# Chunked attention of one layer: both heads of a pair group by group, one split and one store for both

## Chip, cores and metric

The kernel runs on one core of a Trainium2 chip. The metric is the time of one launch on the device, in microseconds, as the median of several runs; the profile is that of one execution.

## The reference

One encoder layer on 1024 tokens of width 1024, in float32: a SwiGLU feed-forward block, then two attention mixers side by side, then a second feed-forward block. The change touches mixer A: attention with 8 heads of 64 columns, in chunks of 64 tokens; a token sees its own chunk and the 8 before it, with a bias for each distance.

```python
def _mixer_a(q, k, v, rel_bias):            # 8 heads of 64
    ...
    s = jnp.einsum('bnqhd,bnkhd->bnhqk', qc, kb) * (Dh ** -0.5)
    ...
    s = jnp.where(valid, s + bias[None, None], -jnp.inf)
    p = jax.nn.softmax(s, axis=-1)
    o = jnp.einsum('bnhqk,bnkhd->bnqhd', p, vb)
    return o.reshape(B, S, H * Dh)
```

After it, o_A is multiplied by a weight, gated, and added to what mixer B gives. Mixer B takes for each token the 256 best keys of an indexer (top-k).

## The kernel before, in words

All engines are programmed as tiles with dependencies; a planner puts the instructions of each engine in an order, by priority and by its own model of time. A tile with a tag has a fixed number of buffers (`bufs`); a new tile of the tag waits until an old one is free. Values are carried as two parts, high and low, so that products come out nearly exact: `split` (line 81) makes both, a ScalarE cast for the high part (line 82) and a VectorE subtraction for the low one (line 83). All DMAs are issued by SyncE (`dma`, line 79), in order.

Mixer A (`mixer_a`, line 698) works on four pairs of heads. For each pair, `load` (line 713) projects queries and keys with 128 columns each, and moves them into the tiles of each head: `qt0`, `qt1` (queries, high and low part stacked), `kk0`, `kk1` (keys, high part twice), `kl0`, `kl1` (low part twice), and `v0`, `v1` (values). Each of these tiles has one buffer. Each head has a bias tile `rb` (line 748), loaded by a DMA, with two small GpSimd memsets (lines 750 and 751); the tag has two buffers.

The loop then goes over the two heads (j), and in a head over four groups (g) of two blocks of 128 tokens (b). For a block, `score_chunks` (line 470, products at 480 and 481) writes the scores into a PSUM bank S (three of them), in one or two chunks; `softmax` (line 632) adds the bias and takes the maximum (VectorE, 639), then the exponential (ScalarE, 641), the reciprocal of its sum (VectorE, 642) and the scaling of the probabilities (GpSimd, 643). A block sees 1, 2, 3, 4, 5, 5, 5, 5 key tiles, so that the four groups have 3, 7, 10 and 10. The probability tile `p` has six buffers, so three groups of a head are on their way at most. `weighted` (line 646) turns the probabilities round on TensorE (665), splits them (tiles `pth`, `ptl`), and multiplies by the values into the bank pv (673). `halves` (line 677) adds the upper and the lower 64 partitions of pv: a ScalarE copy to the tile `half` (683) and a VectorE add to `ot` (684). `split` then makes the tile `os`, and a DMA stores it into `oa_d`. For head 0 this is on partitions 0 to 63, for head 1 on 64 to 127.

Two kinds of other work are woven in. `step` (in `filler`, line 990) is called after each block with its number of key tiles: it pays 0.34 filler steps for each (`pump`, line 134: six products of a projection, the next pair's `load` first, then tiles of the gates), and 0.2 steps of the top-k search. Both are planned at lower priority: the filler 250 instructions later, the search 5000 later. At the end of a pair the kernel pumps until the next pair's `load` is complete. When the stage is over, its pool is closed and the projections of mixer B (`proj_b`, line 788) begin in the same space.

Of the kernel before, what the change touches and what calls it, by code (L numbers as in the profile page):

```python
# [9 lines left out]
F32 = mybir.dt.float32  # L10
F32R = mybir.dt.float32r
# [8 lines left out]
P = 128  # L20
SEQ = 1024
D = 1024
NT = SEQ // P
# [3 lines left out]
HD = 64  # L27
# [10 lines left out]
SPAN_A = 640  # L38
# [5 lines left out]
class Layer:  # L44
# [653 lines left out]
    def mixer_a(self, hh, hl, w_in, va_d, oa_d, step):  # L698
        nc = self.nc
        pool, es = self.open("mxa", bufs=1)  # L700
# [39 lines left out]
        for pr in range(4):  # L740
            qt, kk, kl, vs = nxt
            nxt = []
            if pr < 3:
                self.finish()
                self.fill.appendleft(load(pr + 1, nxt))
            for j in range(2):
                r = j * HD
                bt = pool.tile([P, SPAN_A], F32, tag="rb", name=self.uid("rb"), bufs=2)
                self.dma(bt, self.io["rel"][2 * pr + j])
                nc.gpsimd.memset(bt[0:HD, SPAN_A - HD:SPAN_A], NEG)  # L750
                nc.gpsimd.memset(bt[HD:P, 0:HD], NEG)
                for g in range(NT // 2):
                    sides = []
                    for b in (2 * g, 2 * g + 1):
                        k0 = max(0, b - 4)
                        w = (b + 1 - k0) * P
                        tok = slice(b * P, (b + 1) * P)
                        span = slice(k0 * P, (b + 1) * P)
                        s = self.score_chunks(w, qt[j][:, tok], kk[j][:, span], kl[j][:, span])
                        p = pool.tile([P, SPAN_A], F32, tag="p", name=self.uid("p"), bufs=6)[:, :w]  # L760
                        sides.append((self.softmax(s, bt[:, SPAN_A - w:], p), k0, b + 1))
                        step(b + 1 - k0)
                    pv = self.bank("pv")
                    self.weighted(pv, sides, lambda k: vs[j][:, k, :], pool, 4)
                    ot = pool.tile([P, 256], F32, tag="ot", name=self.uid("ot"))[r:r + HD]
                    os_ = pool.tile([P, 2, 256], F32R, tag="os", name=self.uid("os"), bufs=1)[r:r + HD]
                    self.halves(ot, pv[:, :256], r, pool)
                    self.split(os_[:, 0, :], os_[:, 1, :], ot)
                    self.dma(oa_d[r:r + HD, pr, :, g * 256:(g + 1) * 256], os_)
            while pr < 3 and not nxt:  # L770
                self.pump(1)
        es.close()
# [352 lines left out]
```

## Time and profile before

| | us |
|---|---|
| median of 3 runs | 2391.39 (2390.85 to 2392.74) |
| profiled execution, device time | 2389.99 |
| its span, first to last instruction | 2388.2 |
| TensorE busy in the span | 2265.6 (95%) |
| VectorE busy | 1517.9 (64%) |
| ScalarE busy | 1010.3 (42%) |
| GpSimd busy | 589.8 (25%) |

The engines of a row are PE (TensorE; PEld is its weight load), DVE (VectorE), ACT (ScalarE), POOL (GpSimd) and SP (SyncE, which issues the DMAs). Starts are microseconds from the start of the span. "L82" is line 82 of the kernel. Mixer A's attention lies between about 984 and 1265 us.

### The profile page before, as it was taken

To read this page: it belongs to the slowest core of one execution; us is meant where nothing else is said; L and a number is where in the kernel's file an instruction comes from. 1 tells how busy PE (TensorE), PEld (TensorE's weight loads), DVE (VectorE), ACT (ScalarE), POOL (GpSimd) and SP (SyncE) were. 2 spreads that over 40 slices of the span, in tenths; PEclk is the share of its full clock that TensorE was granted. 3 is DMA by queue.
4 is the path that set the end of the run, shared out by engine and by line. 5 is a ranking of instruction groups with operands and counts; after the bars stand their busy time and mean duration, and the time that the engine had idled before them with its cause. 6 is when DMAs were issued, how large, how long until landed. Compare 5 with 4: busy or idle time off the path is not lost. (4 is left out here: it accounts for less than half of the span.)

```text
span 2388.2 us, 30574 instructions
## 1 busy us (share of the span) xinstructions
PE 2265.6 (95%) x10928; PEld 1893.1 (79%) x10928; DVE 1517.9 (64%) x2917; ACT 1010.3 (42%) x1971; POOL 589.8 (25%) x492
## 2 busy tenths in 40 slices
PE   4999999999998999899998999999799999999998
PEld 3877777778887988687778888878688888878886
DVE  7555555456657459798895378677655555546565
ACT  5444444410104454667743377633444444431012
POOL 6433333100005000223220043221733343300000
PEclk7999999999999999899999999999799999999999
DMA  4233333354414023455523241373233333354331
GB/s 134 89 106 106 106 106 106 106 203 159 159 71 146 1 80 98 131 127 136 126 71 103 87 159 49 112 250 110 89 106 115 106 106 106 106 218 169 132 142 71
DMA packets 204217, 280.82 MB, mean 118 GB/s; under 512 B 12064, under 2 KB 150304, under 8 KB 203552
## 3 DMA queue, kind: packets, MB, share of 16 engines
q1 hardware_dynamic: 204064, 278.86, 35.9%
q8 instruction: 86, 1.41, 0.3%
q14 instruction: 67, 0.55, 0.1%
HBM read 186.55 MB, written 79.69 MB: 111 GB/s over the span
## 5 line engine op out<-in xcount | busy, mean ns | idle before, releaser
L226 DVE SCALAR_TENSOR_TENSOR x<-S,x 128x512 f32<-128x512 f32 x400 | 270.6, 689 | 201.6 <-PE S L118 200.8
L83 DVE TENSOR_TENSOR wop<-raw,wop 128x512 fp32r<-128x512 f32 x210 | 150.3, 723 | 204.5 <-ACT wop L82 203.9
L82 ACT CAST whi<-raw 128x1024 fp32r<-128x1024 f32 (+1 forms) x90 | 85.6, 974 | 413.9 <-PE S L118 335.8
L335 PE MATMUL mm<-bigA,wop 128*128 128x512 f32 (+1 forms) x736 | 236.4, 384 | 10.6 <-ACT e L357 10.6
L335 PE MATMUL S<-bigA,wop 128*128 128x512 f32 (+1 forms) x736 | 235.1, 382 | 5.3 <-POOL wop L83 4.1
L118 PE MATMUL S<-wlo,goh 128*128 128x512 f32 x608 | 236.8, 389 | 0.0
L118 PE MATMUL S<-whi,gol 128*128 128x512 f32 x608 | 236.7, 389 | 0.0
L118 PE MATMUL S<-whi,goh 128*128 128x512 f32 x608 | 232.9, 393 | 1.9 <-DVE bigB L83 1.5
L82 ACT CAST wop<-raw 128x512 fp32r<-128x512 f32 x224 | 137.4, 625 | 103.7 <-PE mm L335 44.9
L335 PEld LDWEIGHTS mm<-bigA,wop 128*128 128x128 f32 x736 | 136.6, 188 | 46.0 <-ACT e L357 19.8
L118 PE MATMUL mm<-bigA,whi 128*128 128x512 f32 x384 | 156.0, 406 | 16.0 <-ACT whi L82 10.0
L83 DVE TENSOR_TENSOR wop<-s,wop 128x512 fp32r<-128x512 f32 x84 | 91.5, 1090 | 115.7 <-ACT wop L82 115.4
L335 PEld LDWEIGHTS S<-bigA,wop 128*128 128x128 f32 x736 | 137.6, 190 | 32.7 <-POOL wop L83 4.5
L118 PE MATMUL mm<-bigA,wlo 128*128 128x512 f32 x384 | 155.2, 405 | 2.1 <-POOL wlo L83 2.1
L118 PE MATMUL mm<-bigB,whi 128*128 128x512 f32 x384 | 154.9, 403 | 0.2 <-DVE bigB L83 0.2
L643 POOL TENSOR_SCALAR p<-p,z 128x640 f32<-128x640 f32 (+7 forms) x128 | 92.5, 726 | 211.8 <-DVE z L642 143.9
L83 POOL TENSOR_TENSOR wlo<-raw,whi 128x1024 fp32r<-128x1024 f32 (+1 forms) x32 | 67.7, 2114 | 301.1 <-ACT whi L82 292.3
L335 PE MATMUL S<-bigB,wop 128*128 128x512 f32 (+1 forms) x368 | 140.4, 382 | 0.1
L335 PE MATMUL mm<-bigB,wop 128*128 128x512 f32 (+1 forms) x368 | 139.8, 380 | 0.0
L118 PEld LDWEIGHTS S<-whi,goh 128*128 128x128 f32 x608 | 114.1, 188 | 31.5 <-DVE x L226 6.3
L309 POOL TENSOR_TENSOR raw<-raw,s 128x512 f32<-128x512 f32 x42 | 54.6, 1300 | 332.4 <-DVE wop L83 332.4
L335 PE MATMUL mm<-b,wop 128*128 128x512 f32 (+1 forms) x552 | 134.5, 381 | 0.0
(257 smaller groups left out, 5375.4 us busy)
## 6 DMA issues: line engine op xcount, KB each, us to landing
raw<-in_ffn_w_in_dram SPq DMA_DIRECT2D x88, 512.0 KB, 4.1
g_d<-g SPq DMA_DIRECT2D x80, 512.0 KB, 5.0
raw<-in_ffn_w_out_dram SPq DMA_DIRECT2D x44, 512.0 KB, 6.9
goh<-g_d SPq DMA_DIRECT2D x38, 512.0 KB, 5.2
gol<-g_d SPq DMA_DIRECT2D x38, 512.0 KB, 6.1
raw<-in_w_in_dram SPq DMA_DIRECT2D x28, 512.0 KB, 5.4
x<-in_x_dram SPq DMA_DIRECT2D x16, 512.0 KB, 7.5
x_d<-x SPq DMA_DIRECT2D x16, 512.0 KB, 2.6
```

The costliest lines, as they stand in the source:

```text
L82: self.nc.scalar.copy(hi, src)
L83: (eng or self.nc.vector).tensor_tensor(lo, src, hi.bitcast(F32), ALU.subtract)
L118: nc.tensor.matmul(out, lhsT=a, rhs=b, start=(i == 0), stop=(i == len(steps) - 1))
L226: nc.vector.scalar_tensor_tensor(xs, po, scale, xs, ALU.mult, ALU.add)
L309: nc.gpsimd.tensor_tensor(out, x, y, op)
L335: nc.tensor.matmul(out, lhsT=l, rhs=r, start=start and j == 0, stop=j == len(steps) - 1, skip_group_check=True)
L643: nc.gpsimd.tensor_scalar(p, p, z, 1.0, ALU.mult, ALU.mult)
```

## The change

The loop over the groups is now the outer one and the loop over the two heads the inner one. Both bias tiles of a pair are made ahead of the groups. The tiles `ot` and `os` belong to the group and not to the head: each head's `halves` writes its 64 partitions of `ot`, and after the second head one `split` on 128 partitions and one store follow. What is computed is the same, and so are the numbers of scores, softmaxes, products and filler steps.

```diff
@@ mixer_a
+            bts = []
             for j in range(2):
-                r = j * HD
                 bt = pool.tile([P, SPAN_A], F32, tag="rb", name=self.uid("rb"), bufs=2)
                 self.dma(bt, self.io["rel"][2 * pr + j])
                 nc.gpsimd.memset(bt[0:HD, SPAN_A - HD:SPAN_A], NEG)
                 nc.gpsimd.memset(bt[HD:P, 0:HD], NEG)
-                for g in range(NT // 2):
+                bts.append(bt)
+            for g in range(NT // 2):
+                ot = pool.tile([P, 256], F32, tag="ot", name=self.uid("ot"))
+                os_ = pool.tile([P, 2, 256], F32R, tag="os", name=self.uid("os"), bufs=1)
+                for j in range(2):
+                    r = j * HD
                     sides = []
                     for b in (2 * g, 2 * g + 1):
...
-                        sides.append((self.softmax(s, bt[:, SPAN_A - w:], p), k0, b + 1))
+                        sides.append((self.softmax(s, bts[j][:, SPAN_A - w:], p), k0, b + 1))
                         step(b + 1 - k0)
                     pv = self.bank("pv")
                     self.weighted(pv, sides, lambda k: vs[j][:, k, :], pool, 4)
-                    ot = pool.tile([P, 256], F32, tag="ot", name=self.uid("ot"))[r:r + HD]
-                    os_ = pool.tile([P, 2, 256], F32R, tag="os", name=self.uid("os"), bufs=1)[r:r + HD]
-                    self.halves(ot, pv[:, :256], r, pool)
-                    self.split(os_[:, 0, :], os_[:, 1, :], ot)
-                    self.dma(oa_d[r:r + HD, pr, :, g * 256:(g + 1) * 256], os_)
+                    self.halves(ot[r:r + HD], pv[:, :256], r, pool)
+                self.split(os_[:, 0, :], os_[:, 1, :], ot)
+                self.dma(oa_d[:, pr, :, g * 256:(g + 1) * 256], os_)
             while pr < 3 and not nxt:
                 self.pump(1)
```

## Rows read from the trace of the kernel before

**Rows 1.** The page, busy time, share of the span and instructions of each engine.

```profile
PE 2265.6 (95%) x10928; PEld 1893.1 (79%) x10928; DVE 1517.9 (64%) x2917; ACT 1010.3 (42%) x1971; POOL 589.8 (25%) x492
```

**Rows 2.** Busy time by stretch: start:end, length, engines (x instructions), clock, DMA share, GB/s.

```profile
984.00:1270.00 286.00, 261.45 (x1406) 219.60 (x1404) 255.41 (x728) 176.03 (x383) 79.86 (x90) 0.97 0.43 113
...
1180.00:1270.00 90.00, 82.29 (x418) 67.37 (x417) 87.65 (x189) 40.83 (x87) 20.96 (x18) 0.96 0.27 81
```

**Rows 3.** Timeline: start, duration, instruction, count, [idle before <-releaser]; end of the stage.

```profile
1268.84 0.69 DVE L629 TENSOR_SCALAR sc<-tkk 128x1024 f32<-128x1024 f16 x1
...
1272.99 1.74 PE L118 MATMUL S<-wb,bigA 128*128 128x384 f32 x4 [4.08 <-ACT wb L82]
```

**Rows 4.** Instructions of the tile os (ns min/median/max); idle ahead of them (us, times).

```profile
L82 ACT CAST os<-ot x32: 397/403/410, 1012.0 to 1262.6; 64x256 fp32r<-64x256 f32 x32
L83 DVE TENSOR_TENSOR os<-ot,os x32: 403/421/2272, 1014.5 to 1264.0; 64x256 fp32r<-64x256 f32 x32
L79 SPq DMA_DIRECT2D oa_d<-os x32: 574/599/2115, 1014.9 to 1264.5; - x32
...
  DVE ot L684: 21.1, 13
  DMA oa_d<-os: 3.1, 3
```

**Rows 5.** Busy time of the tile os alone in one stretch: VectorE, then ScalarE.

```profile
1180.00:1270.00 90.00, 8.30 (x11) 4.04 (x10) 0.96 0.27 81
```

**Rows 6.** Timeline of ScalarE: four of its 32 copies of half.

```profile
1009.97 0.37 ACT L683 COPY half<-pv 64x256 f32<-64x256 f32 x1 [0.22 <-PE pv L673]
...
1127.55 0.36 ACT L683 COPY half<-pv 64x256 f32<-64x256 f32 x1
...
1136.08 0.37 ACT L683 COPY half<-pv 64x256 f32<-64x256 f32 x1
...
1255.71 0.36 ACT L683 COPY half<-pv 64x256 f32<-64x256 f32 x1
```

**Rows 7.** Timeline of TensorE, two stalls; and ten microseconds by stretch around the second.

```profile
994.25 0.79 PE L118 MATMUL mm<-bigA,whi 128*128 128x512 f32 x1 [4.63 <-ACT whi L82]
...
1092.48 0.58 PE L673 MATMUL pv<-pth,v 128*128 128x256 f32 x1 [3.51 <-ACT pth L82]
...
1090.00:1100.00 10.00, 7.38 (x36) 6.54 (x36) 7.81 (x27) 7.19 (x16) 3.18 (x2) 0.83 0.46 98
```

**Rows 8.** Timeline of SyncE's DMA issues between the second and the third pair.

```profile
1094.76 1.20 SPq L79 DMA_DIRECT2D kk<-pwhi  x2
...
1102.03 0.46 SPq L79 DMA_DIRECT2D kk<-pwhi  x1
...
1107.68 1.33 SPq L79 DMA_DIRECT2D kl<-pwlo  x1
...
1125.61 0.34 SPq L79 DMA_DIRECT2D v<-va_d  x1
```

**Rows 9.** Timeline of TensorE there: last score, next scores, last product of the values.

```profile
1101.84 0.28 PE L481 MATMUL S<-kl,qt 128*128 128x256 f32 x1
...
1106.87 0.28 PE L481 MATMUL S<-kl,qt 128*128 128x256 f32 x1
...
1125.31 0.27 PE L673 MATMUL pv<-ptl,v 128*128 128x128 f32 x1
```

**Rows 10.** DMA issues from 984 to 1270: count, KB each, median us to landing.

```profile
kl<-pwlo SPq DMA_DIRECT2D x14, 256.0 KB, 4.8
...
v<-va_d SPq DMA_DIRECT2D x6, 512.0 KB, 3.6
rb<-in_rel_dram SPq DMA_DIRECT2D x6, 320.0 KB, 4.6
```

**Rows 11.** Timeline of GpSimd there: scaling of the second and the third block.

```profile
1112.04 0.48 POOL L643 TENSOR_SCALAR p<-p,z 128x256 f32<-128x256 f32 x1 [3.94 <-PE S L480]
...
1117.63 1.25 POOL L643 TENSOR_SCALAR p<-p,z 128x384 f32<-128x384 f32 x2
```

## Prediction

> **What bounds the kernel now.** I read the engine totals first [rows 1]: TensorE is busy 2265.6 of 2388.2 us, VectorE 1517.9, ScalarE 1010.3. TensorE is the bound over the whole run, and the change takes nothing from TensorE. So the change can only pay by shortening stretches in which TensorE stands idle, and only in the stage it touches. I then read the busy time of that stage [rows 2]. Mixer A runs from the first score at 984 us to the last store at about 1264.5 us; from 984 to 1270 TensorE is busy 261.45 of 286 us, so 24.5 us are idle, and that is the ceiling of any gain. VectorE is busy 255.41 of the same 286. Its last 90 us are different from the rest: from 1180 to 1270 VectorE is busy 87.65 of 90 while TensorE is busy 82.29. There VectorE is the bound, because the last steps of the top-k search have piled up in front of the attention's own subtractions; the last top-k instruction starts at 1268.84 [rows 3]. After that the next projection starts with TensorE idle for 4.08 us [rows 3]. A shorter VectorE queue in these 90 us moves that start, and everything behind it; TensorE's idle there, 90 - 82.29 = 7.7 us, is the most it can give.
>
> Next, the instructions that the change removes, by their tile [rows 4]. There are 32 ScalarE casts (median 403 ns), 32 VectorE subtractions (median 421 ns, but up to 2272 ns) and 32 stores, each on 64 partitions. ScalarE waited 21.1 us for VectorE ahead of 13 of the casts and 3.1 us for an earlier store ahead of 3. Of VectorE's 32 subtractions, 11 lie between 1180 and 1270, and they took 8.30 us in sum [rows 5].
>
> Last, the rhythm of the stage, from ScalarE's copies of the output half [rows 6], one per head and group, 32 in all. The first stands at 1009.97 and the last at 1255.71: 245.74 / 31 = 7.93 us for one group of one head, and groups with 3 key tiles take hardly less than groups with 10.
>
> **The change part by part.**
>
> *Split and store once per group.* Half of the casts, subtractions and stores go: 16 of each. An instruction on 128 partitions and the same 256 columns replaces two on 64. How long it takes is not shown for this tile; I take the same 0.40 and 0.42 us, since the columns are the same (bound: double, which would remove the gain of this part entirely). ScalarE is then freed of 16 x 0.403 = 6.4 us and VectorE of 16 x 0.421 = 6.7 us. Where this lands matters. Of the 11 subtractions in the VectorE-bound stretch about 5.5 go: 5.5 x 0.421 = 2.3 us by the median, 8.30 / 2 = 4.15 us by what they took there. The long ones are single instructions caught behind something else, which will then catch another instruction, so I take the median: **-2.3 us**, all of it on the path. In the rest of the stage VectorE is not the bound, and the 10.5 subtractions that go there (4.4 us) and the shorter ScalarE waits help only where TensorE stands idle for the attention chain, as in the 3.51 us at 1092.48 for a ScalarE cast [rows 7]. Bounds 0 to -4.4 us; I take **-1 us**, near the lower end, since such idle is a small part of that stretch. The 16 stores that go cost no engine but SyncE's queue; nobody on the path waits for their data inside the stage, so nothing is counted for them.
>
> *Both heads group by group: the buffers of a pair.* The tiles qt, kk, kl and v of each head have one buffer. Before, head 0's were free half a pair before the next pair needs them, and head 1's were free at the end of the pair but needed only half a pair later. After, all are free at the end and needed at the beginning. For head 0 nearly nothing changes: its kk and kl loads are issued at 1094.76 and after [rows 8], since they wait for the projection of the next K, not for the buffer; the last group of head 0 would now end one group interval, 7.9 us, ahead of the pair's last score at 1101.84 [rows 9], which is 1093.9. For head 1 the loads follow the pair's last score: kk at 1102.03, and the last kl is issued from 1107.68 to 1109.01 [rows 8]. A kl load lands 4.8 us after its issue [rows 10], so between 1112.5 and 1113.8; I take 1113.1. When is it needed? Head 1's first block becomes the third block of the new pair. In the trace the second block was scored at 1106.87 and scaled on GpSimd at 1112.04, 5.2 us later, and the third was scaled at 1117.63 [rows 9, 11], because the probabilities have six buffers and have to be used up first. Scored at 1113.1, the third block would be scaled at 1118.3, 0.7 us late. Three pair boundaries: 2 us. TensorE has projection work beside it; I count **+1.5 us**, bounds 0 (the loads land as the buffers free) to the full delay of the score, 1113.1 - 1106.9 = 6.2 us each, 18.6 us in all, where nothing covers it.
>
> The v tile of head 1 is free at 1125.31, after the last product of the pair [rows 9]; its load is issued at 1125.61 [rows 8] and lands 3.6 us later [rows 10], about 1129.2. After the change it is needed after head 0's first group of the new pair, one interval later: from 1127.55 to 1136.08 that took 8.5 us [rows 6]. So 0, with a bound of 3.9 us each, 11.7 us in all, were the next product to follow at once. The two bias tiles (rb) have two buffers and now both turn over at the boundary; they land in 4.6 us [rows 10] with 7.9 us to spare for head 0, and later than kl for head 1 only if SyncE puts them behind it. The GpSimd memsets wait for them in order, and what is queued behind there is the scaling of the probabilities; I put this in the same 6.2 us bound.
>
> *The order of sizes.* The groups of one head cover 3, 7, 10 and 10 key tiles. Before, a pair runs 3, 7, 10, 10, 3, 7, 10, 10; after, 3, 3, 7, 7, 10, 10, 10, 10. The number of filler steps is the same (they are paid per key tile), but the light half of a pair pays 20 x 0.34 = 6.8 steps and the heavy half 13.6. At a uniform pace the light half leaves TensorE more room than it is paid for. Filler that lags behind (it is planned later than the attention) evens this out. I take 0, bounds 0 to one stall like that of 3.51 us in each pair, 14 us.
>
> *The sum:* -2.3 - 1 + 1.5 = -1.8 us. The profiled execution took 2389.99 us (span 2388.2), so 2388.2; the median of the runs, 2391.39, lies 1.4 us above the profiled one, so I forecast **2389.6 us**. That lies within 0.2% (4.8 us), which is about what a measurement of this kernel can tell from no change.
>
> **The rivals.**
>
> *Faster: VectorE is the true bound of the whole stage.* VectorE is busy 89% of it and ScalarE's in-order queue loses 21.1 us waiting for VectorE ahead of the casts [rows 2, 4]. Then the full price of all terms holds: -4.15 - 4.4 = -8.6 us, less half of the boundary's cost, about **2383 us**. Against it: only the last 90 us show VectorE at 97%.
>
> *Slower: the boundary becomes a hole.* Head 1's reload stands where before head 0's finished work bridged it. It decides from the point at which the six probability buffers are used up before 1113 on the trace's clock, for then VectorE, ScalarE and TensorE's attention work all wait together. Price: 3 x 6.2 = 18.6 us uncovered, less the gain of 3.3: **2406 us**; half covered, 9.3 - 3.3 = +6, **2397 us**. For it: head 1's six loads keep SyncE busy from 1102 to 1109 (seven issues with a store, the first and the last in [rows 8]), and TensorE's clock was granted at 0.83 in a stretch with a stall of 3.5 us [rows 7], so a hole costs more than itself. Against it: the uniform pace of 7.9 us covers 6.2. The Trainium skill (Trainium Kernel Development and Optimization, Best Practices) says to double-buffer so that DMA overlaps compute; with one buffer per tile, two heads in turn were in effect such a double buffer, and the change gives it up. By that rule alone this rival would be the forecast; the rows above show 6 us of transfer against 8 us of other work.
>
> *Slower: the regrouping starves the filler.* Light groups in a row leave TensorE idle as at 994.25, where the first groups of the stage met 4.63 us without a weight tile ready [rows 7], and the K projection of the next pair, pushed into the heavy half, ends later. One such stall in each of the four pairs, 4 x 3.5 = 14, less 3.3: +10.7 us, **2402 us**.
>
> *The change does nothing.* The removed work was off the path and the reload is covered: **2391 us**. It counts as the same outcome as my forecast.
>
> **How the numbers follow.** Forecast and no effect together 0.40; faster rival 0.31; hole at the boundary 0.17; regrouping 0.12. So faster 0.31, same 0.40, slower 0.29. The range: from 2381 (the faster rival with the boundary free, -8.6, and some 2 us for the different plan behind the stage) to 2402 (half a hole and the regrouping). It leaves out some 2 in 10: the full hole and both slower rivals together. For the forecast alone it would be 2386.6 to 2396.
>
> **What would show each step.** Right: 16 casts and subtractions of os at about 0.40 and 0.42 us on 128 partitions; in the 90 us ahead of the last top-k instruction VectorE still near 97%, and that instruction some 2 to 4 us earlier; the first score of head 1 in a pair held by kl for less than 2 us, with TensorE busy. Wrong: TensorE idle of several us with kl, v or rb named as the releaser right after a pair's last score, granted clock below 1 there; or more TensorE idle in the first four half-groups of each pair; or an os instruction on 128 partitions that takes twice as long.

## The result and the profile after

The changed kernel takes 2410.22 us (median; 2408.74 to 2411.62) beside 2391.57 us before on the same chip: a ratio of 1.0077, with an interval of 1.0064 to 1.009. It is slower by 18.65 us. The forecast was 2389.6 us, no change, with 2402 as the upper end. The forecast and the range both missed.

The profiled execution's span grew from 2388.2 to 2408.2 us, by 20.0. The first page row shows that TensorE's instruction count is the same, and that 16 instructions each went from VectorE and ScalarE [rows 1 for before].

```profile
PE 2275.2 (94%) x10928; PEld 1896.6 (79%) x10928; DVE 1505.4 (63%) x2901; ACT 1002.7 (42%) x1955; POOL 593.7 (25%) x492
```

To find the place of the 20 us I cut both spans at the same four instructions: mixer A's first score, the first projection product that reads the attention output (oa), the first product of the second feed-forward block (it reads wop), and the first product of the next block. "Stage" below is always the stretch from the first of these to the second.

| stretch, us | before | after | difference |
|---|---|---|---|
| start to mixer A's first score | 984.4 | 985.7 | +1.3 |
| mixer A with the filler beside it (the stage) | 411.4 | 414.4 | +3.0 |
| mixer B and the merge | 299.6 | 300.7 | +1.1 |
| second feed-forward block | 464.7 | 479.0 | **+14.3** |
| rest, to the end of the profile | 228.1 | 228.4 | +0.3 |

Nearly three quarters of the loss lie in a stage whose code the diff does not touch. Two stretches by busy time (columns as in [rows 2]), first of before, then of after:

```profile
984.40:1395.80 411.40, 378.94 (x2052) 330.08 (x2050) 307.47 (x919) 231.92 (x538) 93.11 (x107) 0.96 0.39 110
1695.40:2160.10 464.70, 453.55 (x2069) 377.25 (x2070) 257.41 (x318) 196.59 (x350) 170.89 (x122) 0.98 0.37 120
```

```profile
985.70:1400.10 414.40, 381.15 (x2056) 332.86 (x2054) 297.04 (x910) 226.90 (x527) 97.36 (x109) 0.95 0.37 109
1700.80:2179.80 479.00, 460.88 (x2068) 377.68 (x2069) 256.74 (x317) 195.24 (x350) 171.57 (x122) 0.98 0.36 117
```

In the stage VectorE lost 10.4 us of work and ScalarE 5.0, and still the stage got 3.0 us longer. In the feed-forward block nothing was added or removed. Its extra 14.3 us are 7.0 us more idle TensorE (18.1 against 11.2) and 7.3 us more busy TensorE over the same products. In the stage the idle time hardly differs (33.3 against 32.5 us); 2.2 of its 3.0 us are busy TensorE, at a mean granted clock of 0.95 instead of 0.96.

**The feed-forward block.** TensorE's waits there have one row that stands out (line waited for: us in total, times, longest), first of before, from 1690 to 2130 us, then of after, from 1695 to 2150:

```profile
PE mm L335 <- ACT e L357: 1.4, 2, 0.7
```

```profile
PE mm L335 <- ACT e L357: 9.2, 20, 0.7
```

The timeline of TensorE shows why. L335 is the line that issues every product of the block. In after, only one product (into S) stands between the end of one accumulation into mm and the next into the same tile; the next one has to wait until ScalarE has copied the tile out (e, L357). The three lines follow each other in the trace:

```profile
1853.63 0.62 PE L335 MATMUL mm<-t,wop 128*128 128x512 f32 x2
1854.08 0.39 PE L335 MATMUL S<-bigA,wop 128*128 128x512 f32 x1
1854.92 0.50 PE L335 MATMUL mm<-bigA,wop 128*128 128x512 f32 x1 [0.45 <-ACT e L357]
```

In before, the twelve products into tp stand between (the line shows the last three), and there is no wait:

```profile
1866.10 0.84 PE L335 MATMUL tp<-b,wop 128*128 128x512 f32 x3
1866.78 0.39 PE L335 MATMUL mm<-bigA,wop 128*128 128x512 f32 x1
```

The products may be added up in any order, and the planner that orders the instructions chose another order for this block. The *first* feed-forward block of before already has the bad order (the same row, from 60 to 500 us): so it costs the kernel before as well, unnoticed.

```profile
PE mm L335 <- ACT e L357: 9.2, 20, 0.7
```

**The changed instructions.** The tile os in after (columns as in [rows 4]):

```profile
L82 ACT CAST os<-ot x16: 392/406/419, 1020.0 to 1276.8; 128x256 fp32r<-128x256 f32 x16
L83 DVE TENSOR_TENSOR os<-ot,os x16: 397/418/495, 1022.4 to 1277.2; 128x256 fp32r<-128x256 f32 x16
L79 SPq DMA_DIRECT2D oa_d<-os x16: 360/370/1044, 1022.9 to 1277.7; - x16
```

Half as many, at 406 and 418 ns on 128 partitions against 403 and 421 on 64 [rows 4]. The store's issue fell from 599 to 370 ns.

**The end of the stage.** The 90 us around the last top-k instruction, and that instruction, which stands at 1275.60 instead of 1268.84 [rows 2, 3]:

```profile
1190.00:1280.00 90.00, 82.61 (x442) 70.03 (x440) 82.26 (x192) 39.82 (x87) 22.00 (x18) 0.96 0.31 100
...
1275.60 0.69 DVE L629 TENSOR_SCALAR sc<-tkk 128x1024 f32<-128x1024 f16 x1
...
1280.85 0.79 PE L118 MATMUL S<-wb,bigA 128*128 128x384 f32 x3 [3.71 <-ACT wb L82]
```

This stretch reaches 3.2 us further past that instruction than the one of before. Cut alike (1186.8 to 1276.8), VectorE is busy 83.97 of 90 us: its share fell from 97% to 93%, and yet the end came 6.8 us later, 5.5 of them in the stage. The attention itself ends later still: the last of the 32 copies of half stands at 1272.10 instead of 1255.71 us. The gain did not go into an earlier end. VectorE waits more, earlier in the stage. These are the groups of VectorE's instructions over the stage (count | busy us, mean ns | idle us before them and its releasers); first before:

```profile
L639 DVE CUSTOM_DVE_ANT_0 p<-S,rb 128x384 f32<-128x384 f32 (+1 forms) x64 | 32.5, 514 | 9.4 <-PE S L481 6.8 <-PE tp L665 2.5
L684 DVE TENSOR_TENSOR ot<-pv,half 64x256 f32<-64x256 f32 x32 | 13.4, 418 | 4.6 <-ACT half L683 4.1
```

and after:

```profile
L639 DVE CUSTOM_DVE_ANT_0 p<-S,rb 128x384 f32<-128x384 f32 (+1 forms) x64 | 32.3, 518 | 24.2 <-PE S L481 11.4 <-issue 6.8 <-PE tp L665 5.1
L684 DVE TENSOR_TENSOR ot<-pv,half 64x256 f32<-64x256 f32 x33 | 13.8, 418 | 13.1 <-ACT half L683 12.6
```

VectorE waits 14.8 us longer ahead of the score subtraction (4.6 of it for the scores, 2.6 for the transposes that free a tile p, 6.8 without a releaser in the profile) and 8.5 us longer for output halves. Part of it stands where the first pair gives over to the second, where VectorE is busy 2.05 of 10 us (the last line is TensorE's):

```profile
1050.00:1060.00 10.00, 8.18 (x34) 6.05 (x33) 2.05 (x4) 4.31 (x8) 2.37 (x1) 0.83 0.76 211
...
1054.65 0.43 DVE L684 TENSOR_TENSOR ot<-pv,half 64x256 f32<-64x256 f32 x1 [5.09 <-ACT half L683]
...
1061.84 0.29 DVE L639 CUSTOM_DVE_ANT_0 p<-S,rb 128x128 f32<-128x128 f32 x1 [4.96 <-issue]
...
1057.21 0.63 PE L118 MATMUL mm<-bigB,whi 128*128 128x512 f32 x1
```

TensorE is busy for 8.18 of these 10 us, most of it with filler. After two waits of 0.49 and 1.30 us its granted clock is 0.50 (the lower of its two levels, 1.2 GHz) from 1057 to 1059.5: there a product of 512 columns takes 0.63 us instead of 0.39 (above), and the products start 0.43 us apart instead of 0.23. The mean granted clock of the 10 us is 0.83.

**The reload.** At the second and third boundary TensorE waits for the key loads of the new pair, as the timeline of TensorE has it:

```profile
1123.44 0.64 PE L480 MATMUL S<-kk,qt 128*128 128x128 f32 x3 [0.36 <-DMA kk<-pwhi]
1125.38 0.47 PE L481 MATMUL S<-kl,qt 128*128 128x128 f32 x2 [0.65 <-DMA kl<-pwlo]
...
1178.56 0.47 PE L481 MATMUL S<-kl,qt 128*128 128x128 f32 x2 [0.89 <-DMA kl<-pwlo]
1183.95 0.47 PE L481 MATMUL S<-kl,qt 128*128 128x128 f32 x2 [0.54 <-DMA kl<-pwlo]
```

and, over the whole stage, in the row that read 0.3 us, once, before:

```profile
PE S L481 <- DMA kl<-pwlo: 4.4, 5, 2.1
```

The longest, 2.1 us, stands at the very start of the stage: the first pair, too, now needs head 1's keys at once.

### The profile page after: what moved, and what is told of

Read it like the earlier page. It is cut to its first block, busy times and chain, and to the rows that moved or that the text cites. A ratio compares the mean times of both kernels' runs of the same rounds, so it can differ in the third digit from the quotient of the medians.

```text
span 2408.2 us, 30467 instructions
## 1 busy us (share of the span) xinstructions
PE 2275.2 (94%) x10928; PEld 1896.6 (79%) x10928; DVE 1505.4 (63%) x2901; ACT 1002.7 (42%) x1955; POOL 593.7 (25%) x492
## 5 line engine op out<-in xcount | busy, mean ns | idle before, releaser
L83 DVE TENSOR_TENSOR wop<-raw,wop 128x512 fp32r<-128x512 f32 x210 | 143.2, 697 | 255.0 <-ACT wop L82 254.7
L335 PE MATMUL mm<-bigA,wop 128*128 128x512 f32 (+1 forms) x736 | 239.0, 388 | 18.4 <-ACT e L357 18.4
L335 PE MATMUL S<-bigA,wop 128*128 128x512 f32 (+1 forms) x736 | 236.3, 383 | 5.3 <-POOL wop L83 4.1
L335 PEld LDWEIGHTS mm<-bigA,wop 128*128 128x128 f32 x736 | 136.5, 188 | 61.2 <-ACT e L357 35.3
L335 PEld LDWEIGHTS S<-bigA,wop 128*128 128x128 f32 x736 | 138.6, 191 | 32.7 <-POOL wop L83 4.5
L83 DVE TENSOR_TENSOR wop<-s,wop 128x512 fp32r<-128x512 f32 x84 | 99.0, 1178 | 81.9 <-ACT wop L82 81.2
L335 PE MATMUL S<-bigB,wop 128*128 128x512 f32 (+1 forms) x368 | 140.9, 383 | 0.1
L335 PE MATMUL mm<-bigB,wop 128*128 128x512 f32 (+1 forms) x368 | 139.7, 380 | 0.0
L335 PE MATMUL mm<-b,wop 128*128 128x512 f32 (+1 forms) x552 | 135.3, 383 | 0.0
```

What stands on the lines that cost most here:

```text
L83: (eng or self.nc.vector).tensor_tensor(lo, src, hi.bitcast(F32), ALU.subtract)
L335: nc.tensor.matmul(out, lhsT=l, rhs=r, start=start and j == 0, stop=j == len(steps) - 1, skip_group_check=True)
```

## The experiments

Two theories stood at the start. One: the loss is a new plan of the untouched feed-forward block, which a disturbance elsewhere can bring; the change itself costs a few us. The rival: the changed stage itself loses it, through the boundary (reload, starved filler), and the rest is an after-effect. In the tables a kernel's ratio is to the kernel before in the same job, whose median was 2392.3 to 2393.6 us.

### Is it the plan of the feed-forward block?

One disturbance without the change, and the product order fixed in both kernels.

*b_rate*: the kernel before, with more filler.

```
-        self.mixer_a(hh, hl, w_in, va_d, oa_d, filler(0.34, topk, 0.2))
+        self.mixer_a(hh, hl, w_in, va_d, oa_d, filler(0.36, topk, 0.2))
```

> The kernel before with its own loops, splits and stores; only the filler is paid 0.36 steps for each key tile instead of 0.34. The planner then puts the second feed-forward block in the same order as in the changed kernel. Replan theory: the 0.45 us waits appear in each of its tiles although no loop was exchanged, and that block takes 9 to 14 us longer than in the kernel before; in all 2400 to 2406 us. Boundary theory: the order of that block is worth nothing, 2391 +- 4 us.

*b_pin* and *a_pin*: before and after, with the products of the second block issued in the order of the program from its second tile on.

```
     def ffn_in(self, w_in, ops, ph, g_d, first, ws):
...
+        prev = [None]
+        pinned = first is None
 
         def product(out, w, b, cols, start):
+            with nullcontext() if prev[0] is None else self.tc.issue_after(prev[0]):
+                last = product_free(out, w, b, cols, start)
+            if pinned and m == 512:
+                prev[0] = last
...
```

(`product_free` is the old `product`, which now returns its last instruction.)

> The kernel before, with one addition: in the second feed-forward block the products on TensorE, from its second tile on, must stand in the order in which they are written. It is the control for the next two runs. Replan theory (most of the 19 us were lost because the planner put the second feed-forward block in another order, one in which TensorE waits 0.45 us in each of its tiles): the kernel before already has an order there without that wait, so 2391 +- 4 us. Boundary theory (the 19 us are lost in mixer A): nothing there depends on this order, so 2391 +- 4 us as well. The run is there for the difference to the next.

> The changed kernel with the same fixed order in the second feed-forward block. Replan theory: the 0.45 us waits there go, and about 14 us of the 20 us of span with them; what is left is what mixer A and the stages behind it lost, 4 to 6 us against the control. Boundary theory: all of it stays, 18 to 20 us against the control.

*b_both* and *a_both*: the same with `pinned = True`, for both blocks.

> The kernel before with the fixed order of the products in both feed-forward blocks. In its trace the first block has the 0.45 us wait in each of its tiles, the second has not. If the wait is a matter of the order alone, the first block gets some 9 us shorter too: 2380 to 2384 us, as long as the new plan of mixer A behind it is no worse than 4 us. If the wait comes from something else in the first block, 2390 us as the control.

> The changed kernel with the fixed order in both feed-forward blocks: 1 to 5 us above the run before, if the direct cost of the change does not hang on one plan of mixer A; 2382 to 2388 us.

| kernel | us | ratio [interval] | stage | second feed-forward |
|---|---|---|---|---|
| b_rate | 2401.70 | 1.0041 [1.0028, 1.0054] | 407.1 | 479.5 |
| b_pin | 2389.89 | 0.9986 [0.9978, 0.9995] | 409.2 | 463.3 |
| a_pin | 2392.58 | 0.9999 [0.999, 1.0008] | 413.0 | 462.4 |
| b_both | 2374.42 | 0.9919 [0.9905, 0.9933] | 411.2 | 461.6 |
| a_both | 2376.27 | 0.9933 [0.9921, 0.9945] | 415.9 | 462.4 |

b_rate has no part of the change; with its amount of filler the planner was known to order the block as in after, so it shows that the order can come without the change, not how often. Its stage even gets shorter, and the feed-forward block takes 479.5 us with the same row of TensorE's waits:

```profile
PE mm L335 <- ACT e L357: 9.2, 20, 0.7
```

With the order fixed, after falls from 2410.22 to 2392.58 us, and before hardly moves. So the new plan of the block is the larger part, **shown** in both directions: it comes without the change (b_rate) and goes with it still there (a_pin). What the change costs by itself is a_pin against b_pin, 2.7 us, and a_both against b_both, 1.9 us; the intervals of both pairs overlap, so its sign is likely, not certain. For a_pin 4 to 6 us above b_pin had been expected.

b_both shows the other thing found on the way: the first block of before gives back 15 us when its products are fixed too, and its row of waits from 60 to 500 us is gone but for one:

```profile
PE mm L343 <- ACT e L366: 0.5, 1, 0.5
```

The forecast for both (2380 to 2384 and 2382 to 2388) was too high: it had priced the bad order by its 9.2 us of waits alone, and the block cost some 15, as the second block does (14.3).

The same mixer code in three executions also tells how far a stage's length can be trusted: 411.4, 409.2 and 411.2 us in before, b_pin and b_both, 414.4, 413.0 and 415.9 in after, a_pin and a_both. A difference of two stages below some 3 us (the 2.9 from 413.0 to 415.9) is thus no more than a hint, and the length of a stage is one execution's.

From here on every kernel has the second block fixed (names in _pin, and nb, na, ng), so that its stage can be compared; g_rate and b_hold as well.

### The two halves of the change, one at a time

*g_pin*: after with the split and the store back inside the loop over the heads, so that only the loops are exchanged. *g_rate* is g_pin with filler 0.36.

```
             for g in range(NT // 2):
-                ot = pool.tile([P, 256], F32, tag="ot", name=self.uid("ot"))
-                os_ = pool.tile([P, 2, 256], F32R, tag="os", name=self.uid("os"), bufs=1)
                 for j in range(2):
...
-                    self.halves(ot[r:r + HD], pv[:, :256], r, pool)
-                self.split(os_[:, 0, :], os_[:, 1, :], ot)
-                self.dma(oa_d[:, pr, :, g * 256:(g + 1) * 256], os_)
+                    ot = pool.tile([P, 256], F32, tag="ot", name=self.uid("ot"))[r:r + HD]
+                    os_ = pool.tile([P, 2, 256], F32R, tag="os", name=self.uid("os"), bufs=1)[r:r + HD]
+                    self.halves(ot, pv[:, :256], r, pool)
+                    self.split(os_[:, 0, :], os_[:, 1, :], ot)
+                    self.dma(oa_d[r:r + HD, pr, :, g * 256:(g + 1) * 256], os_)
```

> The loops exchanged as in the change, but each head still splits and stores its own 64 partitions; the fixed order in the second feed-forward block as in the control. If exchanging the loops costs and the common split pays what my sum said (3.3 us), this is 3 us slower than the changed kernel with the fixed order. If the common split is worth nothing, the two are equal within 1.5 us, and both 4 to 6 us above the control. If the common split is what costs, this equals the control.

> Exchanged loops with a split and a store for each head, as before (2405 us), but the filler paid 0.36 instead of 0.34 steps. If the exchange of the loops without the common split costs 13 to 17 us by its nature, again 2400 to 2408 us. If the 2405 was one unlucky plan of mixer A, 2390 to 2398 us.

*m_pin*: the loops of before, but one split and store for both heads; the four outputs of a pair are held in one of the five raw weight buffers until head 1 is done. *b_hold*: the outputs held there too, but split and stored per head as before. First the edit of m_pin, then that of b_hold.

```
+            ots = self.raw()
...
-                    self.halves(ot, pv[:, :256], r, pool)
-                    self.split(os_[:, 0, :], os_[:, 1, :], ot)
-                    self.dma(oa_d[r:r + HD, pr, :, g * 256:(g + 1) * 256], os_)
+                    ot = ots[:, g * 256:(g + 1) * 256]
+                    self.halves(ot[r:r + HD], pv[:, :256], r, pool)
+                    if j == 1:
+                        os_ = pool.tile([P, 2, 256], F32R, tag="os", name=self.uid("os"), bufs=1)
+                        self.split(os_[:, 0, :], os_[:, 1, :], ot)
+                        self.dma(oa_d[:, pr, :, g * 256:(g + 1) * 256], os_)
```

```
+            ots = self.raw()
...
-                    ot = pool.tile([P, 256], F32, tag="ot", name=self.uid("ot"))[r:r + HD]
+                    ot = ots[r:r + HD, g * 256:(g + 1) * 256]
```

> The old loops (head by head), with only the split and the store made common: head 0's outputs of a pair wait in one weight buffer until head 1's are there, then one split and one store on 128 partitions for each group; fixed order in the second feed-forward block. My sum: 2 to 3.3 us faster than the control (2387). By the gap between the last two runs with exchanged loops (12.6 us for the common split alone): 2377 to 2382. If the gap was scatter of the planner: within 3 us of the control, either way.

> Control for the common split in the old loops: each head splits and stores for itself as before, but its outputs are kept in the same weight buffer that the common split occupied (one of five, held for the whole pair). If that run's 2397 us came from the missing weight buffer, this is 2396 to 2401 us, and the common split is worth 0 to 3 us; if the buffer is worth nothing, 2388 to 2392 us, and the common split in the old loops costs 5 to 8 us by itself.

| kernel | us | ratio [interval] | stage |
|---|---|---|---|
| g_pin, loops exchanged alone | 2405.22 | 1.0052 [1.0038, 1.0065] | 426.6 |
| g_rate | 2403.24 | 1.0045 [1.0031, 1.0059] | 425.3 |
| m_pin, common split alone | 2397.23 | 1.0016 [1.0007, 1.0025] | 418.3 |
| b_hold, its control | 2406.97 | 1.0057 [1.0043, 1.0071] | 431.0 |

The two halves pull apart much more than the sum had it. Exchanging the loops alone costs 15.3 us (2405.22 - 2389.89; the stage 17.4), and the common split then gives 12.6 of it back (2405.22 - 2392.58; the stage 13.6). More filler is no cure for the exchange.

m_pin alone would have misled: slower than b_pin by 7.3 us, which none of its three forecasts had, as if the common split cost something. Its control, itself 6 us above its forecast, shows that holding the outputs in a weight buffer is what costs, 17 us from b_pin to b_hold, and that the common split under the same handicap gains 9.7 us. A weight buffer fewer shows where one expects it: TensorE waits 17.2 us in the stage of b_hold for the tiles of the filler's weights, 8.7 in that of b_pin. First b_hold:

```profile
PE mm L118 <- ACT whi L82: 9.7, 6, 4.2
PE mm L118 <- POOL wlo L83: 7.5, 5, 2.3
```

then b_pin:

```profile
PE mm L118 <- ACT whi L82: 6.3, 3, 4.5
...
PE mm L118 <- POOL wlo L83: 2.4, 3, 1.7
```

### What does the exchange cost: the reload?

*nb*, *na*, *ng*: b_pin, a_pin and g_pin with the moves into qt, kk, kl and v left out for all pairs but the first.

```
...
-            for j in range(2):
...
+            for j in range(2 if pr == 0 else 0):
                 r = j * HD
                 self.dma(qt[j][r:r + HD, :], qh[r:r + HD, :])
...
+            if pr > 0:
+                out += self.first_pair
+                return
...
+            self.first_pair = list(out)
```

> The kernel before with the fixed order in the second feed-forward block, and mixer A computed with the first pair's queries, keys and values for all four pairs: the projections of the other pairs still run, but their moves into qt, kk, kl and v are left out, so nothing waits for the buffers at the pair boundaries. Control for the next run; 2386 to 2391 us by either theory, since the old loops have half a pair for these loads.

> The same leaving out of the moves in the changed kernel (fixed order in the second feed-forward block). If what the change still costs in mixer A (2.7 us of time, 3.8 us from the first score to the first product of the gated branch) comes from the reload at the pair boundaries, it is gone: equal to the control without moves, or up to 4 us faster. If it comes from the order of the group sizes, 2 to 5 us above that control remain.

> Exchanged loops with a split and a store for each head, and without the moves into qt, kk, kl and v of the later pairs (all pairs use the first pair's); fixed order in the second feed-forward block. If the 13 to 17 us of the exchanged loops come from the reload at the boundaries, this is as fast as the other two without moves: 2381 to 2388 us. If they come from the order of the group sizes or from the chain through ot and os, 2393 to 2400 us.

| loops and split | stage with moves | without | moves cost | time without |
|---|---|---|---|---|
| before (b_pin, nb) | 409.2 | 405.8 | 3.4 | 2381.10 |
| exchanged, common split (a_pin, na) | 413.0 | 406.3 | 6.7 | 2386.93 |
| exchanged alone (g_pin, ng) | 426.6 | 416.4 | 10.2 | 2393.93 |

In the stage, after without the reload is 0.5 us from before without it; of the 3.8 us by which a_pin's stage is longer, the reload is 3.3. That part of the prediction's mechanism fits, at a size near the scatter of the stage. But in time na stays 5.8 us above nb, where the forecast for the reload as the cause was equal or up to 4 us faster: by the times it did not come true. Of the 7.5 us between the two profiled executions 4.6 lie behind the stage, in mixer B and the merge, and 1.9 in the feed-forward block, so the omission moved other work there as well; these two kernels are to be read by the stage. nb lies 5 us below its own forecast: the old loops pay for the moves too. The bias tiles are loaded as before in all three. And without any reload the exchange still costs 10.6 us (416.4 - 405.8), which the common split then takes away (10.1).

The two parts of the exchange differ in kind. First the stage of g_pin, then of ng and nb:

```profile
986.00:1412.60 426.60, 386.92 (x2056) 335.30 (x2054) 304.80 (x926) 234.83 (x543) 97.65 (x109) 0.94 0.37 106
```

```profile
986.60:1403.00 416.40, 375.85 (x2055) 327.88 (x2053) 314.97 (x926) 232.61 (x543) 97.14 (x109) 0.97 0.26 78
```

```profile
986.30:1392.10 405.80, 373.40 (x2055) 328.19 (x2053) 309.27 (x926) 233.50 (x543) 95.95 (x109) 0.97 0.27 80
```

The moves make TensorE slower, not more idle: from ng to g_pin its busy time grows by 11.1 us over the same products, with the mean granted clock at 0.94 instead of 0.97, and its idle time (40.6 and 39.7 us) does not. The rest of the exchange, from nb to ng, is mostly idle TensorE, 8.2 of 10.6 us, at the same granted clock.

### Is the rest of it the order of sizes, or the single buffers?

*o_pin* and *go_pin*: a_pin and g_pin with light and heavy groups in turn.

```
-            for g in range(NT // 2):
+            for g in (0, 2, 1, 3):
```

> The changed kernel with the fixed order in the second feed-forward block, and the groups of a pair taken in the order 0, 2, 1, 3, so that light and heavy groups alternate (3, 3, 10, 10, 7, 7, 10, 10 key tiles). If the direct cost of the change comes from four light half-groups in a row, 2 to 5 us faster than in the written order (2392.6): 2388 to 2390. If not, 2391 to 2395 us.

> Exchanged loops with a split and a store for each head (2405 us in the written order of groups) with the groups in the order 0, 2, 1, 3. If the order of sizes is what the exchange of the loops costs, 2393 to 2398 us. If it is the chain through the single buffers of ot and os, or something else, 2402 to 2408 us.

*g2_pin*: g_pin with two buffers each for ot and os; to make room, the probabilities' transposes have three instead of four.

```
+                    ot = pool.tile([P, 256], F32, tag="ot", name=self.uid("ot"), bufs=2)[r:r + HD]
+                    os_ = pool.tile([P, 2, 256], F32R, tag="os", name=self.uid("os"), bufs=2)[r:r + HD]
-                    self.weighted(pv, sides, lambda k: vs[j][:, k, :], pool, 4)
+                    self.weighted(pv, sides, lambda k: vs[j][:, k, :], pool, 3)
```

> Exchanged loops with a split and a store for each head (2405 us), now with two buffers each for ot and os, paid for by three instead of four buffers for the transposed probabilities (which cost nothing in the old loops); fixed order in the second feed-forward block. If the exchange costs by the chain of both heads through the single buffers of ot and os, 2388 to 2396 us. If not, 2402 to 2408 us.

| kernel | us | ratio [interval] | stage |
|---|---|---|---|
| o_pin | 2388.81 | 0.9983 [0.9974, 0.9992] | 412.1 |
| go_pin | 2407.02 | 1.0059 [1.0046, 1.0073] | 430.5 |
| g2_pin | 2408.33 | 1.0068 [1.0053, 1.0082] | 429.8 |

Neither explains the exchange: go_pin's stage is 3.9 us longer than g_pin's, not shorter, and a second buffer for ot and os, bought with a buffer of the transposes, changes nothing for the better. On the changed kernel the order in turn takes 3.8 us off the time (2392.58 - 2388.81), within the 2 to 5 forecast for it, and the two intervals hardly overlap. The two profiled executions lie only 0.9 us apart, as their stages do, so where the 3.8 us were gained is not to be read; the sizes may well account for the 2.7 us of a_pin, but they don't for the exchange alone.

What remains is a row that divides these six kernels by their loops, VectorE's wait ahead of the score subtraction (p<-S,rb) in the stage: 9.7 us in b_pin and 7.9 in nb; 16.1 in g_pin, 21.4 in a_pin, 16.0 in ng, 15.8 in na. First nb, then ng (idle is the third column):

```profile
L648 DVE CUSTOM_DVE_ANT_0 p<-S,rb 128x384 f32<-128x384 f32 (+1 forms) x64 | 32.3, 516 | 7.9 <-PE S L490 6.8 <-PE tp L674 1.0
```

```profile
L648 DVE CUSTOM_DVE_ANT_0 p<-S,rb 128x384 f32<-128x384 f32 (+1 forms) x64 | 32.1, 518 | 16.0 <-PE S L490 11.0 <-issue 3.0 <-PE tp L674 1.7
```

With the loops exchanged VectorE stands 8 us longer ahead of its score subtractions, reload or no reload (from nb to ng 4.2 of it for the scores, 3.0 without a releaser in the profile). That is close to the 10.6 us in size, but g_pin's wait is smaller than a_pin's although its stage is 13.6 us longer, and the kernels that hold a weight buffer have a long wait with the loops of before as well (16.4 us in m_pin, 19.6 in b_hold). It is a sign, not the cause. TensorE's largest wait in both kernels is for the bank pv, until VectorE's add into ot has read it, first nb, then ng:

```profile
PE pv L682 <- DVE ot L693: 7.5, 5, 3.1
```

```profile
PE pv L682 <- DVE ot L693: 12.1, 6, 2.8
```

In na it is 4.5 us. The bank pv and the tile half have one buffer each, and no run gave them a second one; against them as the whole cause stands that the same wait is only 2.8 us in g_pin. What makes the exchange slow beyond the reload **stays open**.

### Kernels faster than both

*m3_both*: the loops of before, one split and store per group for both heads, but with four tiles of its own for the outputs (no weight buffer is taken), the transposes with three buffers, and both feed-forward blocks fixed. *b3_both* is its control: only the three buffers and the fixed blocks.

```
+            ots = [pool.tile([P, 256], F32, tag="ot", name=self.uid("ot"), bufs=4) for _ in range(NT // 2)]
...
+                    self.halves(ots[g][r:r + HD], pv[:, :256], r, pool)
+                    if j == 1:
+                        os_ = pool.tile([P, 2, 256], F32R, tag="os", name=self.uid("os"), bufs=1)
+                        self.split(os_[:, 0, :], os_[:, 1, :], ots[g])
+                        self.dma(oa_d[:, pr, :, g * 256:(g + 1) * 256], os_)
```

> Old loops with a common split and store whose outputs wait in four small buffers of their own, paid for by one buffer less (three instead of four) for the transposed probabilities; fixed order of the products in both feed-forward blocks. By the gap between the two kernels with a held weight buffer (10 us for the common split alone), 2362 to 2368 us, faster than every other kernel here; by my sum, 2371 to 2374 us; if three buffers are too few, above its control's time minus 3.

> Control for the run before: old loops, a split and a store for each head, three instead of four buffers for the transposed probabilities, fixed order in both feed-forward blocks. 2374 to 2378 us if the fourth buffer is not needed, more if it is.

*o3_both*: the changed kernel with groups in turn, two buffers for ot and os, three for the transposes, both blocks fixed.

```
-            for g in range(NT // 2):
+            for g in (0, 2, 1, 3):
+                ot = pool.tile([P, 256], F32, tag="ot", name=self.uid("ot"), bufs=2)
+                os_ = pool.tile([P, 2, 256], F32R, tag="os", name=self.uid("os"), bufs=2)
```

> The changed kernel with groups in the order 0, 2, 1, 3, two buffers for ot and os, three for the transposed probabilities, and the fixed order in both feed-forward blocks. Sum of what was measured apart: 2376.3 - 3.8 for the order of groups, 0 for the rest: 2370 to 2374 us, level with the old loops so pinned and a little above the old loops with a common split (2368).

| kernel | us | ratio [interval] | stage |
|---|---|---|---|
| m3_both | **2368.07** | 0.9898 [0.9884, 0.9911] | 405.0 |
| b3_both | 2372.73 | 0.9913 [0.9899, 0.9926] | 407.7 |
| o3_both | 2373.61 | 0.9922 [0.9906, 0.9938] | 413.6 |

m3_both has the lowest median of all, 25.3 us below before. Most of that is the fixed order of products, which b_both has as well. The common split itself, without the exchange, is worth 4.7 us by the medians and 2.7 by the stage; the two intervals overlap, so that it helps at all is likely but not settled. o3_both lies where its sum had put it, 2.7 us below a_both. The stage of m3_both beside that of b3_both has less work, VectorE -11.6 us and ScalarE -7.4. The os subtractions are 5.1 us of it (15.6 to 10.5); part of the rest are other instructions that fall outside the cuts (22 fewer on VectorE, 16 of them by the change):

```profile
967.80:1372.80 405.00, 374.24 (x2051) 327.66 (x2049) 292.39 (x903) 226.47 (x522) 93.94 (x107) 0.97 0.38 111
```

```profile
969.00:1376.70 407.70, 378.71 (x2055) 328.78 (x2054) 303.95 (x925) 233.90 (x542) 95.02 (x109) 0.97 0.39 110
```

## Why the prediction was wrong, step by step

**What bounds the kernel.** That the change could move the time only in the stage that it touches was the step that failed. The plan behind the stage stood in the range with "some 2 us", on the fast side; it measured 14.3 us of loss in one block. With it failed the step that only idle TensorE can be gained or lost: half of the 14.3 us (7.3) is busy TensorE over the same products, and from b_pin to g_pin 9.0 of 17.4 us of stage are (386.92 - 377.88). The row that would have warned was in the trace of before: its first feed-forward block loses 9.2 us in 20 waits that its second block, with the same code, does not have. One code, two plans: so the good plan of the second block was luck, and a change ahead of it could lose it. Which of the two plans would come was not to be read from any row; the least that it would cost was, 9.2 us of waits.

**One instruction on 128 partitions for two on 64.** Right: 418 and 406 ns. The work taken from VectorE was undersized: 19.48 us of os subtractions (32 at 609 ns on the mean) became 6.72 in the stage, 12.8 us against the 6.7 that the medians gave. The step that the long ones would catch another instruction was wrong as a rule for the stage: the longest os subtraction is now 495 ns, it had been 2272 [rows 4], and VectorE's total over the run fell by 12.5 us, so it was not passed on. In m3_both, with the loops of before, the long ones are there again (up to 2558 ns), so the step is not wrong everywhere.

**The common split, -3.3.** The sign is right: it is -13.6 us of stage with the loops exchanged, -12.7 with the held buffer, -2.7 with the loops of before and buffers of their own. The size depends on what else is short, and the sum's value fits only the last case. A term read from the kernel before was priced there, but the change first moves the stage to a place where the term weighs four times as much.

**The end of the stage earlier by 2 to 4 us.** Wrong: 6.8 us later (5.5 without the later start), with VectorE at 93%. VectorE's work in the last 90 us did fall, but the attention had fallen behind by then: the first pair alone takes 65.1 us from its first to its last copy of half, 57.3 before. That the boundaries held it up is argued from the waits above, not shown by a run.

**The reload, +1.5 (bounds 0 to 18.6).** Mechanism right: the keys are late and TensorE is held by kl for less than 2 us each at the boundaries, 2.4 us in all (2 had been worked out before the cover was taken off). By the kernels without moves it is worth 3.3 us of stage, near the scatter. A missed place: the first pair, 2.1 us. The bias tiles, which the prediction left in the bound, hold GpSimd longer, 19.4 us in 5 waits instead of 10.3 in 6; what that is worth no run shows. That the next product of the values would wait for v: no such row among TensorE's waits in after, as forecast. The Trainium skill (Trainium Kernel Development and Optimization, Best Practices) says to double-buffer so that DMA overlaps compute. The trace agrees in sign: the moves cost the stage 3.4 us with two heads in turn and 6.7 without.

**The order of sizes, 0 (bound 14).** Open: taking it back gave 3.8 us by the medians on the changed kernel, and cost 1.8 on g_pin.

**What no term held.** The exchange of the loops costs 17.4 us of stage alone, of which the moves account for 6.8 (10.2 - 3.4). 10.6 us have no term in the sum and no cause here. That the sum (-1.8) lies only 4.5 us from the direct cost (+2.7) is luck: two errors of more than 10 us cancelled, 15.9 in the exchange (17.4 against 1.5) and 10.3 in the common split (13.6 against 3.3).

**The rivals.** "Hole at the boundary", 2397 to 2406, came nearest to the time, but for another reason than its own: VectorE does wait 5.09 and 4.96 us at the first boundary, with filler at 0.63 us a product, but all of it nets to +3 us of stage. "VectorE is the true bound" did not come true: VectorE has 10.4 us less work in the stage, and the stage is longer. But with the loops exchanged, taking that work away gives 10 to 14 us of stage, so there the chain through ScalarE and VectorE does count. "Starved filler" found little support: more filler on the exchanged loops gave 1.3 us of stage, and groups in turn helped the changed kernel alone.

## What to carry to other kernels

Where a planner orders the instructions, a change has a second price: the order that it brings elsewhere. Look in the trace before for one piece of code that runs twice with different waits, price the worse plan for both, and fix that order before anything else is measured; here this was worth more (15 us) than the better half of the change (4.7 us by the medians, m3_both). And test both halves of a change singly, each with a control for what it needs to be built (the held buffer cost 17 us, and hid a gain of 9.7 us): two large effects of opposite sign can look like a small one.

## What the runs showed of the hardware that was not expected

An elementwise subtraction of 64 x 256 elements on VectorE, 421 ns in the median, took up to 2272 ns in before [rows 4] and 609 on the mean; on 128 partitions in after, the same kind of instruction took 418 in the median and at most 495. In m3_both, with the same 128 partitions, the mean was 659 again, so the 128 partitions alone don't decide it; what held the long ones up was not tested.

Where the first pair gives over to the second, TensorE in after is busy 8.18 of 10 us, because filler takes the attention's place, but part of it with products that start 0.43 instead of 0.23 us apart: the busy share hides what the granted clock (0.83) tells. The same holds for a whole stage: from ng to g_pin TensorE's busy time grows by 11.1 us over the same products, at 0.94 instead of 0.97.
